# A two-block fp32 transformer on one core: the scan's state products on column halves, one bank per attention head, and the order of two mixers

## The chip, the cores and the metric

The kernel runs on 1 core of one Trainium2 chip. The metric is the device time of one execution in microseconds, as the median of several runs.

## What is computed

256 tokens x of width 1024 (and 256 context tokens) go through two blocks in fp32. The first block has two layers. Its layer 0 mixes with a bidirectional gated delta rule (8 heads of 64, chunks of 64 tokens) and with latent attention (MLA, 8 heads); its layer 1 with neighbourhood attention (8 heads) and grouped-query attention (8 heads on 2 key heads). Each layer ends in a gated FFN. The second block has two layers whose mixer joins sparse attention over chosen keys, a causal 31-tap convolution and a pooling. Cut to what the change touches:

```python
# delta rule, per chunk, head and direction
v_new = u_i - w_i @ s
o_i   = qd_i @ s + qk_i @ v_new
s     = s * gl_i + kd_i.T @ v_new

# attentions of the first block, per head
p = softmax(q @ k.T * scale + bias)        # 256 queries, 512 keys
o = p @ v

# second block's mixer
scores = index(qi, ki, wi)                 # per token half; top 64 of up to 256 keys
o_att  = softmax(q @ k.T + mask(top_k(scores))) @ v
y      = conv31(a * sigmoid(g)) + conv_b
o_conv = silu(layernorm(y)) @ conv_pw
out    = concat(o_att, o_conv, o_pool) @ w_out
```

## The kernel before

The program is one long piece of straight code. A scheduler sets the order of the instructions on each engine from the order of the code and its own estimate of durations; each engine then runs its instructions strictly in that order. Products with weights are made of three matmuls on parts of each number (mm3, L554 to L556); the weights stream in as 512 KB transfers, and ScalarE (L270) and VectorE or GpSimd (L272) make the two parts. PSUM has eight banks. Each stage divides them by kind: the layer-0 mixer has three "g" (reached by aux()), two "s", and one each of "tp", "po", "gv"; the layer-1 mixer and the second block's mixers have two "acc" (acc()), two "s", two "tp", one "aux" and one "po". A new tile of a kind waits until its bank's last reader is done.

*Scan (gdn_run, 264 to 396 us).* Four rounds; in each, the forward and the backward direction take one tile of two chunks. gdn_operands makes, by products of 64 by 64 (L1159, L1161) and transposes (L1164), the tile's u, w, decayed keys kd and decayed queries Q. gdn_state then goes through the tile's two chunks, one on partitions 0 to 63, one on 64 to 127 (the "row half" a): w·S for four head pairs (L1193), v_new on VectorE (gvn, L1196), the state update kd·v_new as four matmuls of 64 rows by 128 columns (L1200), of whose 128x128 results only the two diagonal 64x64 blocks are added to S, and Q·v_new as eight matmuls on one quarter of the array (L1211). The backward direction starts after the forward one's chunks in the code. MLA's pairs 0 and 1 and the modulation products are mixed in by the scheduler; MLA's pairs 2 and 3 come behind (396 to 441 us).

*attend.* For a pair of heads and 128 queries: scores into two banks, row maximum on VectorE (L674), exponentials and their sums on ScalarE (p, L676), four transposes per head into a bank of another kind (L679), copies to SBUF (pt, L682 on VectorE, L684 on ScalarE), the products with v (L690). sums_row makes a row of reciprocal sums (L698, L700). In MLA and in the layer-1 mixer p and pt have two buffers each (K.np).

*Layer-1 mixer (l1_mixer).* linear_tok makes blocks (chunk, token tile) of the input product; consume then issues what hangs on them. The order is: chunks 2, 1 and half of 0, na(0), chunk 4 and half of 3, na(1), the late transposes of the grouped-query keys and queries (late, through pairs_T, L1350, each through the one aux bank), gqa(0), gqa(1). na(t) and gqa(t) are four pairs each for 128 queries.

*Second mixers (s_mixer, twice).* Index scores and top-k for token half 1 (choose(1), VectorE, writes the mask at L1630), linears, qkv, then in this order: conv (128 matmuls on diagonal weights that ScalarE makes, L1531, in two banks, the bias as a 32nd tap), choose(0), the pooling, finish (layer norm from L1542 to L1547, transposes L1550, scaling and tanh, the pointwise product L1560, split L652 and L653), att(1), att(0). s_attend takes one head pair's scores on top of mask products (L1645), with p and pt in two buffers each.

Of the kernel before, what the change touches and what calls it, by code (L numbers as in the profile page):

```python
# [10 lines left out]
F32 = mybir.dt.float32  # L11
# [653 lines left out]
def attend(K, score, v, po, rb, c, kinds=("s", "s", "tp", "tp")):  # L665


    nc = K.nc
    sm = cut(K, [128, 2], F32, "sm", 4)
    pts = []  # L670
    for hh, ps in enumerate(score([bank(K, kinds[0]), bank(K, kinds[1])])):
# [9 lines left out]
        if hh:  # L681
            nc.vector.tensor_copy(pt[:, :n], tp[:, :n])  # L682
        else:
            nc.scalar.copy(pt[:, :n], tp[:, :n])  # L684
# [103 lines left out]
def l0_mla(K, O):  # L788
# [49 lines left out]
    wq = None  # L838
    for pair in range(4):
# [21 lines left out]
        for t in range(4):  # L861
            n = 256 if t < 2 else 512

            def score(pss):
                tk = slice(t * 128, (t + 1) * 128)
                for hh in range(2):
# [4 lines left out]
                   ("s", "g", "tp", "g") if late else ("s", "s", "tp", "tp"))  # L871
        nc.scalar.copy(O[:, pair, :], rb)
        nc.vector.tensor_tensor(O[:, pair, :], po, O[:, pair, :], op=ALU.mult)

# [309 lines left out]
def gdn_state(K, d, first, t, a, u, wq, kd, Q, S):  # L1184
    nc = K.nc
    r = slice(64 * a, 64 * a + 64)
    o = slice(64 - 64 * a, 128 - 64 * a)
# [13 lines left out]
    pSv = pS.rearrange("p (q c) -> p q c", q=4)  # L1201
    for hh in range(2):
        x = slice(hh * 64, hh * 64 + 64)
        if first:
            nc.vector.tensor_copy(S[x, :, x], pSv[x, :, x])
        else:
            nc.gpsimd.tensor_tensor(S[x, :, x], S[x, :, x], bc(K.glc[d][x, t, a, :], [64, 4, 64], 2), op=ALU.mult)
            nc.vector.tensor_tensor(S[x, :, x], S[x, :, x], pSv[x, :, x], op=ALU.add)
# [145 lines left out]
def l1_mixer(K, W, oh, ol):  # L1354
# [44 lines left out]
    def na(t):  # L1399
        po, rb = bank(K, "po"), aux(K)  # L1400
        for pair in range(4):
            def score(pss):
                out = pair_scores(K, (qh[:, pair], ql[:, pair]), (kh[:, pair], kl[:, pair]), 512, tok(t), pss)
                for hh in range(2):
# [5 lines left out]
                   ("s", "acc", "tp", "acc") if t == 1 and pair >= 1 else ("s", "s", "tp", "tp"))  # L1410
        attended(K, po, rb, oh, ol, 0, t)

    def gqa(t):
        po, rb = bank(K, "po"), aux(K)
        for pair in range(4):
            g = pair // 2

            def score(pss):
                return pair_scores(K, (gqh[:, pair], gql[:, pair]), (gkh[:, g], gkl[:, g]), 512, tok(t), pss)
            attend(K, score, lambda hh, j: vg[:, j, g * 64:g * 64 + 64], po, rb, pair * 128, ("s", "acc", "tp", "acc"))  # L1420
# [49 lines left out]
def s_conv(K, i, oh, ol):  # L1470
# [46 lines left out]
    def taps(c):  # L1517

        for j in range(32):
            if j % 3 == 0:  # L1520
                dg = cut(K, [128, 3, 128], F32, "dg", 2)
            nc.scalar.mul(dg[:, j % 3, :], K.ident, dw[:, i, c, j:j + 1] if j < 31 else dwb[:, i, c:c + 1])
            yield j, dg[:, j % 3, :]

    def conv():

        ps = [bank(K, "po"), bank(K, "tp")]
        for c in range(2):
            for j, dg in taps(c):
                for t in range(2):  # L1530
                    nc.tensor.matmul(ps[t][:, c * 128:c * 128 + 128],  # L1531
                                     yp[:, c, t * 128 + j:t * 128 + j + 128] if j < 31 else ones, dg,
                                     start=(j == 0), stop=(j == 31))
        return ps

    def finish(ps):
        y = cut(K, [128, 2, 256])
        back = acc(K)
# [94 lines left out]
def s_attend(K, g, t, qh, ql, kh, kl, mask, U, O):  # L1633
# [6 lines left out]
    for hh in range(2):  # L1640
        r = slice(hh * 64, hh * 64 + 64)
        ps = bank(K, "s")
# [6 lines left out]
        p, pt = cut(K, [128, 512], F32, "p", 2), cut(K, [128, 512], F32, "pt", 2)  # L1649
        tp = bank(K, "tp")  # L1650
# [6 lines left out]
        po = bank(K, "po")  # L1657
# [10 lines left out]
def s_mixer(K, W, i, xh, xl, oh, ol):  # L1668
# [37 lines left out]
    with Pool(K, "ix"):  # L1706
# [252 lines left out]
def layer1(K, h):  # L1959
# [5 lines left out]
    with Pool(K, "l1o"):  # L1965
# [8 lines left out]
        closed(K, K.px)  # L1974
        W.drop()
# [40 lines left out]
def second(K, h):  # L2016
# [10 lines left out]
    for i in range(2):  # L2027
        with Pool(K, "so"):
# [8 lines left out]
            closed(K, K.px)  # L2037
            W.drop()
# [132 lines left out]
```

## Time and profile before

| | |
|---|---|
| median of 3 runs | 2148.2 us (2139.5 to 2151.42) |
| the profiled execution | 2141.66 us; its span 2139.8 us |
| mean granted TensorE clock | 0.955 |
| PE busy | 2003.9 us (94%) |
| VectorE, ScalarE, GpSimd busy | 1318.1, 923.5, 241.2 us |

The span is the time from the first to the last instruction of the profiled execution. PE is the matmul engine; its clock has two levels, 2.4 GHz (granted clock 1.00) and 1.2 GHz (0.50), and a stretch's granted clock is the mean over it. DVE is VectorE, ACT is ScalarE, POOL is GpSimd. A row of a timeline gives start and duration in us, then engine, line, operation, tiles, sizes and, in brackets, the idle time ahead of it with what ended it. A matmul of fp32 is two instructions, and a matmul's duration includes the time it needs to drain, so the price of a group is read from its start to the next group's start.

### The profile page before, as it was taken

To read this page: it belongs to the slowest core of one execution; us is meant where nothing else is said; L and a number is where in the kernel's file an instruction comes from. 1 tells how busy PE (TensorE), PEld (TensorE's weight loads), DVE (VectorE), ACT (ScalarE), POOL (GpSimd) and SP (SyncE) were. 2 spreads that over 40 slices of the span, in tenths; PEclk is the share of its full clock that TensorE was granted. 3 is DMA by queue.
4 is the path that set the end of the run, shared out by engine and by line. 5 is a ranking of instruction groups with operands and counts; after the bars stand their busy time and mean duration, and the time that the engine had idled before them with its cause. 6 is when DMAs were issued, how large, how long until landed. Compare 5 with 4: busy or idle time off the path is not lost.

```text
span 2139.8 us, 31171 instructions
## 1 busy us (share of the span) xinstructions
PE 2003.9 (94%) x11656; PEld 1629.7 (76%) x11656; DVE 1318.1 (62%) x2737; ACT 923.5 (43%) x1614; POOL 241.2 (11%) x312
## 2 busy tenths in 40 slices
PE   6989799899999999799798999998999999989998
PEld 3768578678878778687466888997788789868886
DVE  5666557767776744637556555574765557577644
ACT  4533444344222234434445443564554345555532
POOL 2120112301000000213101001110200021020000
PEclk9999899899999999899689999998999999989999
DMA  8344640234686633213024654521556535155662
GB/s 282 94 114 115 197 139 26 69 100 128 190 261 209 191 105 99 91 61 102 25 89 147 188 187 149 159 87 48 189 179 194 168 108 147 31 167 177 187 187 69
DMA packets 186952, 291.90 MB, mean 136 GB/s; under 512 B 28472, under 2 KB 75704, under 8 KB 186800
## 3 DMA queue, kind: packets, MB, share of 16 engines
q1 hardware_dynamic: 172720, 272.54, 40.8%
q0 software_dynamic: 5472, 16.13, 2.2%
q10 hardware_dynamic: 8608, 1.23, 0.4%
q8 instruction: 92, 1.51, 0.3%
q14 instruction: 60, 0.49, 0.1%
HBM read 281.44 MB, written 8.41 MB: 135 GB/s over the span
## 4 chain that ended last, share of the span: by engine, by line
PE 85%; DVE 6%; DMA 4%; ACT 3%; issue 2%; ACTq 0%; POOL 0%; SPq 0%; DVEq 0%; POOLq 0%
PE acc L554 19%; PE acc L556 19%; PE acc L555 19%; PE s L554 2%; PE s L555 2%; PE s L556 2%; PE po L690 2%; PE tp L891 2%; PE po L1531 1%; PE tp L1531 1%; DMA wraw<-in_w_mod_dram 1%; PE gv L373 1%; DVE wlo L272 1%; PE tp L679 1%; PE aux L729 1%
## 5 line engine op out<-in xcount | busy, mean ns | idle before, releaser
L272 DVE TENSOR_TENSOR wlo<-wraw,whi 128x512 fp32r<-128x512 f32 (+4 forms) x772 | 482.0, 669 | 293.6 <-ACT whi L270 276.6
L270 ACT CAST whi<-wraw 128x1024 fp32r<-128x1024 f32 (+4 forms) x420 | 413.4, 990 | 483.7 <-PE acc L556 200.5
L554 PE MATMUL acc<-whi,u 128*128 128x512 f32 (+3 forms) x1320 | 510.2, 389 | 17.8 <-ACT u L306 11.2
L556 PE MATMUL acc<-whi,u 128*128 128x512 f32 (+3 forms) x1320 | 507.0, 386 | 1.2 <-DVE u L307 1.2
L555 PE MATMUL acc<-wlo,u 128*128 128x512 f32 (+3 forms) x1320 | 508.1, 387 | 0.0
L554 PEld LDWEIGHTS acc<-whi,u 128*128 128x128 f32 x1320 | 252.1, 191 | 68.0 <-ACT u L306 13.7
L556 PEld LDWEIGHTS acc<-whi,u 128*128 128x128 f32 x1320 | 251.8, 191 | 51.4 <-DVE u L307 3.6
L555 PEld LDWEIGHTS acc<-wlo,u 128*128 128x128 f32 x1320 | 252.3, 191 | 48.3 <-DVE wlo L272 1.4
L554 PE MATMUL acc<-u,whi 128*128 128x512 f32 (+1 forms) x480 | 170.0, 361 | 1.8 <-ACT u L306 1.7
L556 PE MATMUL acc<-u,wlo 128*128 128x512 f32 (+1 forms) x480 | 170.0, 358 | 0.0
L555 PE MATMUL acc<-u,whi 128*128 128x512 f32 (+1 forms) x480 | 169.5, 355 | 0.2 <-DVE u L307 0.2
L272 POOL TENSOR_TENSOR wlo<-wraw,whi 128x512 fp32r<-128x512 f32 (+1 forms) x68 | 84.0, 1266 | 431.0 <-ACT whi L270 431.0
L432 DVE SCALAR_TENSOR_TENSOR msum<-mraw,u,msum 128x512 f32<-128x512 f32 x140 | 100.8, 747 | 13.7 <-DMA mraw<-in_w_mod_dram 12.7
L554 PEld LDWEIGHTS acc<-u,whi 128*128 128x128 f32 x480 | 90.1, 189 | 17.0 <-issue 2.6
L555 PEld LDWEIGHTS acc<-u,whi 128*128 128x128 f32 x480 | 90.7, 189 | 15.1 <-issue 1.7
L556 PEld LDWEIGHTS acc<-u,wlo 128*128 128x128 f32 x480 | 90.3, 189 | 15.1 <-issue 1.7
L307 DVE TENSOR_TENSOR u<-aux,u 128x512 fp32r<-128x512 f32 (+2 forms) x96 | 59.5, 632 | 40.6 <-ACT u L306 40.4
L306 ACT CAST u<-aux 128x512 fp32r<-128x512 f32 (+2 forms) x96 | 50.3, 542 | 52.4 <-PE aux L729 36.5
L554 PE MATMUL acc<-whi,dxh 128*128 128x512 f32 x176 | 69.7, 396 | 1.9 <-ACT dxh L306 1.9
L555 PE MATMUL acc<-wlo,dxh 128*128 128x512 f32 x176 | 69.6, 396 | 0.0
L556 PE MATMUL acc<-whi,dxl 128*128 128x512 f32 x176 | 68.7, 396 | 0.0
L307 DVE TENSOR_TENSOR dxl<-u,dxh 128x1024 fp32r<-128x1024 f32 x22 | 26.7, 1224 | 52.8 <-ACT dxh L306 52.8
(511 smaller groups left out, 3103.1 us busy)
## 6 DMA issues: line engine op xcount, KB each, us to landing
wraw<-in_w_up_dram SPq DMA_DIRECT2D x64, 512.0 KB, 4.0
wraw<-in_w_down_dram SPq DMA_DIRECT2D x64, 512.0 KB, 3.9
mraw<-in_w_mod_dram SPq DMA_DIRECT2D x56, 512.0 KB, 4.9
wraw<-in_w_ffn_down_dram SPq DMA_DIRECT2D x44, 512.0 KB, 3.8
wraw<-in_w_mod_dram SPq DMA_DIRECT2D x40, 512.0 KB, 5.7
wraw<-in_w_ffn_gate_dram SPq DMA_DIRECT2D x48, 256.0 KB, 3.0
wraw<-in_w_ffn_up_dram SPq DMA_DIRECT2D x48, 256.0 KB, 3.6
wraw<-in_w_ffn_gate_dram SPq DMA_DIRECT2D x20, 512.0 KB, 3.7
```

The costliest lines, as they stand in the source:

```text
L270: self.K.nc.scalar.copy(hi, raw)
L272: e.tensor_tensor(lo[:, k], raw[:, k], hi.bitcast(F32)[:, k], op=ALU.subtract)
L306: (hi_eng or nc.scalar.copy)(hi, src)
L307: nc.vector.tensor_tensor(lo, src, hi.bitcast(F32), op=ALU.subtract)
L373: nc.tensor.matmul(ps[32 * j:32 * j + 32, :], K.cl[:, g + k, :], raw[:, k, :], start=(g + k < 4), stop=(g + k >= 4))
L432: nc.vector.scalar_tensor_tensor(accs[s], raw[:, k, :], c, accs[s], op0=ALU.mult, op1=ALU.add)
L554: mm(ps, ah, bh, start=start, stop=False)
L555: mm(ps, ah, bl, start=False, stop=False)
L556: mm(ps, al, bh, start=False, stop=stop)
L690: nc.tensor.matmul(po[hh * 64:hh * 64 + 64, c:c + 128], v(hh, j), pts[hh][0][:, j * 128:(j + 1) * 128], start=(j == 0), stop=(j == nj - 1))
L891: nc.tensor.matmul(tp[:, t * 128:(t + 1) * 128], x[:, t // 2, t % 2 * 128 + j:t % 2 * 128 + j + 128], dg[j], start=(j == 0), stop=(j == 4))
L1531: nc.tensor.matmul(ps[t][:, c * 128:c * 128 + 128], yp[:, c, t * 128 + j:t * 128 + j + 128] if j < 31 else ones, dg, start=(j == 0), stop= ...
```

## The change

In the scan, the state update is eight products of 64 by 64 that alternate between the two column halves of the array and fill 256 columns of one bank. Both directions' operands come ahead of both directions' state steps. The query products of both directions are issued alternately, head by head, into one bank, on two diagonal quarters of the array. In attend, a head's transposes go into the bank that held its scores (tp = bks[hh]), so that a head uses one bank, and pairs rotate over the kinds; p and pt get three buffers in MLA and six in the layer-1 mixer. There the linears all come first, then na(0), the late transposes, na(1), gqa. In the second mixers att(1) is ahead of the convolution, finish and att(0) behind it; s_attend uses one bank per head too, with p and pt in four buffers, and the convolution fits in one bank, with its bias as one matmul ahead of the taps.

```diff
 def attend(K, score, v, po, rb, c, kinds, copies="SV"):
+    bks = [bank(K, kinds[0]), bank(K, kinds[1])]
+    for hh, ps in enumerate(score(bks)):
...
-        tp = bank(K, kinds[2 + hh])
+        tp = bks[hh]
...
-def gdn_state(K, d, first, t, a, u, wq, kd, Q, S):
+def gdn_state(K, d, first, t, a, u, wq, kd, S):
...
         nc.vector.tensor_tensor(vn[r], u[r], ps[r], op=ALU.subtract)
-    pS, po = aux(K), aux(K)
+        gdn_o(K, t, a, slice(64 - 64 * a, 128 - 64 * a), ps)
+    pS = aux(K)[:, :256].rearrange("p (q c) -> p q c", q=4)
     for p in range(4):
-        c = slice(p * 128, (p + 1) * 128)
-        nc.tensor.matmul(pS[:, c], kd[r, c], vn[r, c], start=True, stop=True)
+        for hh in range(2):
+            c = slice(p * 128 + hh * 64, p * 128 + hh * 64 + 64)
+            nc.tensor.matmul(pS[hh * 64:hh * 64 + 64, p, :], kd[r, c], vn[r, c], start=True, stop=True)
...
-    for h in range(8):
-        hs = slice(h * 64, h * 64 + 64)
-        nc.tensor.matmul(po[o, hs], Q[r, h, :], vn[r, hs], start=True, stop=True)
-    if not first:
-        gdn_o(K, t, a, o, ps)
-    gdn_o(K, t, a, o, po)
+    return vn
...
 def gdn_run(K):
     for i in range(4):
-        for d in range(2):
-            t = i if d == 0 else (1, 0, 3, 2)[i]
-            ops = gdn_operands(K, d, t)
-            for a in ((0, 1) if d == 0 else (1, 0)):
-                gdn_state(K, d, i == 0 and a == d, t, a, *ops, K.S[d])
+        ts = [i, (1, 0, 3, 2)[i]]
+        ops = [gdn_operands(K, d, ts[d]) for d in range(2)]
+        for s in range(2):
+            vns = []
+            for d in range(2):
+                u, wq, kd, Q = ops[d]
+                a = s ^ d
+                vns.append((64 * a, Q, gdn_state(K, d, i == 0 and s == 0, ts[d], a, u, wq, kd, K.S[d])))
+            po = aux(K)
+            for h in range(8):
+                hs = slice(h * 64, h * 64 + 64)
+                for a, Q, vn in vns:
+                    K.nc.tensor.matmul(po[64 - a:128 - a, hs], Q[a:a + 64, h, :], vn[a:a + 64, hs], start=True, stop=True)
...
@@ l1_mixer @@
-    linear_tok(K, W, xs, w, chunks, [(2, 0), (2, 1), (2, 2), (2, 3), (1, 0), (1, 1), (1, 2), (1, 3), (0, 2), (0, 3)],
-               consume)
-    na(0)
-    linear_tok(K, W, xs, w, chunks, [(4, t) for t in range(4)] + [(3, 2), (3, 3)], consume)
-    na(1)
-    for f in late:
-        f()
-    for t in range(2):
-        gqa(t)
+    linear_tok(K, W, xs, w, chunks, [(2, 0), (2, 1), (2, 2), (2, 3), (1, 0), (1, 1), (1, 2), (1, 3), (0, 2), (0, 3),
+                                     (4, 0), (4, 1), (4, 2), (4, 3), (3, 2), (3, 3)], consume)
+    closed(K, K.px)
+    W.drop()
+    with Pool(K, "at"):
+        K.np = 6
+        na(0)
+        for f in late:
+            f()
+        na(1)
+        for t in range(2):
+            gqa(t)
...
@@ s_mixer @@
         qkv()
-        cv = conv()
-        choose(0)
-        pool_out(0)
-        pool_out(1)
-        finish(cv)
-        att(1)
-        att(0)
+        with Pool(K, "at"):
+            att(1)
+            cv = conv()
+            choose(0)
+            pool_out(0)
+            pool_out(1)
+            finish(cv)
+            att(0)
```

Three places on PE, where the scheduler's order shows what moved. A row reads: line, operation, tile written, tiles read, size, and how many.

The end of na(1) in the layer-1 mixer, before: the last products with v (L690), the late transposes (L1350; lkd are doubled keys), then the first scores of gqa (L710).

```order
L690 MATMUL po_9058<-pt_9239,u_8091 64x128
L1350 MATMUL aux_9257<-const_id_75,lkd_8760 128x128 x2
L1350 MATMUL aux_9262<-const_id_75,lkd_8810 128x128 x2
L1350 MATMUL aux_9267<-const_id_75,lkd_8866 128x128 x2
L1350 MATMUL aux_9272<-const_id_75,lkd_8922 128x128 x2
L1350 MATMUL aux_9277<-const_id_75,lx_8977 128x128 x4
L710 MATMUL s_9294<-u_8087,u_8089 128x512
L710 MATMUL acc_9295<-u_8087,u_8089 128x512
```

The same place now, in the middle of na(1) (L709 scores, L681 transposes of p, L689 products with v, L1366 late transposes):

```order
L709 MATMUL acc_9208<-u_8107,u_8109 128x512
L709 MATMUL acc_9208<-u_8108,u_8109 128x512
L709 MATMUL acc_9208<-u_8107,u_8110 128x512
L681 MATMUL tp_9116<-const_id_75,p_9141 128x128 x4
L681 MATMUL s_9161<-const_id_75,p_9177 128x128 x4
L1366 MATMUL aux_9078<-const_id_75,lkd_8585 128x128 x2
L709 MATMUL tp_9253<-u_8107,u_8109 128x512
L709 MATMUL tp_9253<-u_8108,u_8109 128x512
L709 MATMUL tp_9253<-u_8107,u_8110 128x512
L681 MATMUL s_9162<-const_id_75,p_9187 128x128 x4
L689 MATMUL po_9112<-pt_9137,u_8115 64x128
```

The late transposes stood in a row; now each stands between the work of several pairs, whose scores are already in three kinds of bank.

The end of qkv in the first of the two second mixers, before (L1531 is the convolution; the s products behind it are the index scores of token half 0):

```order
L555 MATMUL acc_12548<-wlo_12517,u_9657 128x384
L556 MATMUL acc_12548<-whi_12516,u_9658 128x384
L1531 MATMUL tp_12615<-dg_12626,u_11691 128x128
L1531 MATMUL po_12614<-dg_12626,u_11691 128x128
...
L1531 MATMUL tp_12615<-dg_12636,u_11691 128x128
L554 MATMUL s_12831<-u_12037,u_12066 128x128
L555 MATMUL s_12831<-u_12038,u_12066 128x128
```

The same place now (L1366 are the transposes of att(1)'s keys and queries, L1677 its mask products, the s products its scores):

```order
L555 MATMUL acc_12544<-wlo_12513,u_9653 128x384
L556 MATMUL acc_12544<-whi_12512,u_9654 128x384
L1366 MATMUL aux_12586<-const_id_75,akd_12576 128x128 x2
L1366 MATMUL aux_12591<-const_id_75,u_11681 128x128 x4
L1366 MATMUL aux_12598<-const_id_75,akd_12584 128x128 x2
L1677 LDWEIGHTS u_11652
L1677 MATMUL s_12614<-u_11685,u_11652 128x256
...
L1366 MATMUL aux_12603<-const_id_75,u_11681 128x128 x4
L554 MATMUL s_12614<-u_12024,u_12026 128x256
L555 MATMUL s_12614<-u_12025,u_12026 128x256
```

The convolution behind the linears is gone from here, and att(1) has taken its place.

The end of the same mixer, before (L1550 and L1560 belong to finish, L1655, L1660 and L729 to the attentions, the last row to w_out):

```order
L1550 MATMUL acc_12955<-const_id_75,lnx_12981 128x128 x2
L1655 MATMUL tp_13109<-const_id_75,p_13107 128x128 x4
L1660 MATMUL po_13057<-u_11685,pt_13048 128x64 x4
L1655 MATMUL tp_13146<-const_id_75,p_13144 128x128 x2
L1560 MATMUL aux_12995<-u_12954,u_11698 128x256
...
L1655 MATMUL tp_13224<-const_id_75,p_13222 128x128 x2
L1660 MATMUL po_13178<-u_11685,pt_13171 128x64 x2
L1660 MATMUL po_13204<-u_11685,pt_13197 128x64 x2
L729 MATMUL aux_13236<-const_id_75,u_12032 128x128 x2
L1660 MATMUL po_13230<-u_11685,pt_13223 128x64 x2
L729 MATMUL aux_13236<-const_id_75,u_12032 128x128 x2
L554 MATMUL acc_13295<-whi_13268,u_11661 128x512
```

The same place now (L1563 is the convolution, L1687 and L1692 are att(0), L1582 and L1592 finish, L728 att(0)'s output):

```order
L1692 MATMUL acc_13196<-u_11681,pt_13190 128x64 x2
L1563 MATMUL po_12737<-dg_12948,u_11687 128x128 x2
L1687 MATMUL tp_13202<-const_id_75,p_13214 128x128 x2
L1692 MATMUL acc_13221<-u_11681,pt_13215 128x64 x2
L1582 MATMUL aux_13077<-const_id_75,lnx_13099 128x128 x2
L1582 MATMUL aux_13077<-const_id_75,lnx_13103 128x128 x2
L1592 MATMUL aux_13117<-u_13076,u_11694 128x256 x2
L1592 MATMUL aux_13122<-u_13076,u_11694 128x256 x2
L728 MATMUL aux_13227<-const_id_75,u_12028 128x128 x4
L554 MATMUL acc_13286<-whi_13259,u_11657 128x512
```

The attentions' last units stood behind the transposes of finish; now they stand ahead of them, and finish has only the four transposes of L728 beside it.

## Rows read from the trace of the kernel before

**Rows 1.** The page: busy time of each engine; the chain's shares by engine.
```profile
PE 2003.9 (94%) x11656; PEld 1629.7 (76%) x11656; DVE 1318.1 (62%) x2737; ACT 923.5 (43%) x1614; POOL 241.2 (11%) x312
...
PE 85%; DVE 6%; DMA 4%; ACT 3%; issue 2%; ACTq 0%; POOL 0%; SPq 0%; DVEq 0%; POOLq 0%
```

**Rows 2.** Windows: length, busy PE, PEld, DVE, ACT, POOL, then PE clock, DMA share, GB/s.
```profile
264.00:396.00 132.00, 124.78 (x1384) 100.10 (x1381) 89.39 (x169) 50.29 (x117) 26.45 (x39) 0.97 0.25 79
376.00:400.00 24.00, 20.46 (x181) 17.35 (x178) 16.21 (x37) 5.06 (x11) 8.69 (x14) 0.73 0.23 69
396.00:441.00 45.00, 40.37 (x252) 28.93 (x250) 34.49 (x66) 23.73 (x57) 10.46 (x14) 0.95 0.23 80
973.00:1105.00 132.00, 113.56 (x646) 78.48 (x646) 83.55 (x207) 58.23 (x121) 25.11 (x40) 0.80 0.14 44
1012.00:1105.00 93.00, 74.56 (x403) 49.28 (x398) 51.15 (x97) 38.32 (x82) 11.20 (x13) 0.72 0.07 22
1050.00:1083.00 33.00, 31.43 (x120) 20.36 (x120) 12.93 (x18) 9.99 (x24) 0.00 (x0) 0.50 0.00 1
1464.00:1490.00 26.00, 19.85 (x94) 17.00 (x92) 12.61 (x43) 7.44 (x23) 1.14 (x2) 0.67 0.03 11
1866.00:1890.00 24.00, 17.85 (x95) 14.94 (x95) 14.57 (x46) 8.94 (x24) 1.14 (x2) 0.77 0.13 41
```

**Rows 3.** Timeline of PE in the scan: start, duration, engine, line, operation.
```profile
279.13 0.68 PE L1161 MATMUL g<-u,gke 64*64 64x64 f32 x16
279.74 0.33 PE L1164 MATMUL g<-const_id,gqe 128*128 128x128 f32 x1
...
284.75 1.14 PE L1211 MATMUL g<-gu,gQ 64*64 64x64 f32 x16
285.82 1.16 PE L1193 MATMUL g<-u,gwq 128*128 128x128 f32 x8
...
289.87 1.16 PE L1200 MATMUL g<-gvn,gkd 64*128 64x128 f32 x8
290.96 0.97 PE L1211 MATMUL g<-gvn,gQ 64*64 64x64 f32 x13
...
291.88 0.98 PE L1159 MATMUL g<-u,u 64*64 64x64 f32 x27
```

**Rows 4.** Groups of L1200 and L1211: count, ns min/median/max, first and last start.
```profile
L1200 PE MATMUL g<-gvn,gkd x112: 272/272/579, 274.0 to 393.1; 64*128 64x128 f32 x112
...
L1211 PE MATMUL g<-gvn,gQ x224: 218/218/363, 275.1 to 395.1; 64*64 64x64 f32 x112
```

**Rows 5.** Waits of PE, 1010 to 1105 us: total, times, longest in us.
```profile
PE tp L679 <- ACT p L676: 6.7, 4, 2.8
```

**Rows 6.** Timeline of PE, 1040 to 1050 us.
```profile
1044.20 0.44 PE L1350 MATMUL aux<-const_id,lkd 128*128 128x128 f32 x2 [0.92 <-DVE u L307]
1045.56 0.44 PE L1350 MATMUL aux<-const_id,lkd 128*128 128x128 f32 x2 [0.92 <-DVE u L307]
```

**Rows 7.** Timelines of PE and DVE at the end of qkv, first second mixer.
```profile
1416.64 0.34 PE L556 MATMUL acc<-whi,u 128*128 128x384 f32 x1
1416.81 0.38 PE L1531 MATMUL tp<-dg,u 128*128 128x128 f32 x2
...
1423.00 0.43 DVE L1630 TENSOR_TENSOR u<-u,const_rest 128x256 bf16<-128x256 f32 x1
```

**Rows 8.** Timelines of DVE and PE at the end of the same mixer.
```profile
1463.92 0.43 DVE L1542 BATCH_NORM_STATS2 bst<-po 128x6 f32<-128x256 f32 x1 [1.08 <-PE po L1531]
...
1467.86 0.53 DVE L1547 TENSOR_SCALAR lnx<-tp,bmv,rsy 128x256 f32<-128x256 f32 x1
...
1481.77 0.42 DVE L653 SCALAR_TENSOR_TENSOR u<-aux,u 128x256 fp32r<-128x256 f32 x1 [2.06 <-ACT u L652]
...
1468.00 0.69 PE L1550 MATMUL acc<-const_id,lnx 128*128 128x128 f32 x2 [3.35 <-DVE lnx L1547]
...
1489.76 0.80 PE L554 MATMUL acc<-whi,u 128*128 128x512 f32 x1 [1.62 <-ACT whi L270]
```

More of the change, by code (lines that the diff above doesn't have):

```diff
@@ L661, in heads_T, with attend @@
     feat_split(K, hi, lo, ps[:, :T * 128], scale)
-def attend(K, score, v, po, rb, c, kinds=("s", "s", "tp", "tp")):
+def attend(K, score, v, po, rb, c, kinds, copies="SV"):
     nc = K.nc
@@ L670, in attend @@
     pts = []
-    for hh, ps in enumerate(score([bank(K, kinds[0]), bank(K, kinds[1])])):
+    bks = [bank(K, kinds[0]), bank(K, kinds[1])]
+    for hh, ps in enumerate(score(bks)):
         n = ps.shape[-1]
@@ L680, in attend @@
         pt = cut(K, [128, 512], F32, "pt", K.np)
[L681 to L684, printed above, removed]
+        (nc.vector.tensor_copy if copies[hh] == "V" else nc.scalar.copy)(pt[:, :n], tp[:, :n])
         pts.append((pt, n // 128))
@@ L838, in l0_mla, with unit @@
     wq = None
+    used = [0]
+    def unit(kinds):
+        used[0] += 2
+        return [kinds[(used[0] + i) % len(kinds)] for i in range(2)]
+    K.np = 3
     for pair in range(4):
@@ L870, in l0_mla @@
             attend(K, score, lambda hh, j: vt[:, j, pair * 128 + hh * 64:pair * 128 + hh * 64 + 64], po, rb, t * 128,
-                   ("s", "g", "tp", "g") if late else ("s", "s", "tp", "tp"))
+                   unit(("s", "s", "tp", "g", "g", "g") if late else ("s", "s", "tp")))
         nc.scalar.copy(O[:, pair, :], rb)
         nc.vector.tensor_tensor(O[:, pair, :], po, O[:, pair, :], op=ALU.mult)
+    K.np = 2
 def gdn_conv(K, W, f0, nf, silu, tensor):
@@ L1409, in na @@
             attend(K, score, lambda hh, j: vn[:, j, pair * 128 + hh * 64:pair * 128 + hh * 64 + 64], po, rb, pair * 128,
-                   ("s", "acc", "tp", "acc") if t == 1 and pair >= 1 else ("s", "s", "tp", "tp"))
+                   unit(), "SS")
         attended(K, po, rb, oh, ol, 0, t)
@@ L1419, in score, with unit @@
                 return pair_scores(K, (gqh[:, pair], gql[:, pair]), (gkh[:, g], gkl[:, g]), 512, tok(t), pss)
[L1420 removed]
+            attend(K, score, lambda hh, j: vg[:, j, g * 64:g * 64 + 64], po, rb, pair * 128, unit())
         attended(K, po, rb, oh, ol, 4, t)
[L1423 to L1431 removed]
+    used = [0]
+    def unit():
+        used[0] += 1
+        return [("s", "acc", "tp")[used[0] % 3]] * 2
+    linear_tok(K, W, xs, w, chunks, [(2, 0), (2, 1), (2, 2), (2, 3), (1, 0), (1, 1), (1, 2), (1, 3), (0, 2), (0, 3),
[10 more added lines that the diff above has]
+            gqa(t)
+        K.np = 2
 def rope2_tables(K, pool):
@@ L1517, in taps @@
     def taps(c):
-        for j in range(32):
+        for j in range(31):
             if j % 3 == 0:
                 dg = cut(K, [128, 3, 128], F32, "dg", 2)
-            nc.scalar.mul(dg[:, j % 3, :], K.ident, dw[:, i, c, j:j + 1] if j < 31 else dwb[:, i, c:c + 1])
+            nc.scalar.mul(dg[:, j % 3, :], K.ident, dw[:, i, c, j:j + 1])
             yield j, dg[:, j % 3, :]
     def conv():
-        ps = [bank(K, "po"), bank(K, "tp")]
+        ps = bank(K, "po")
+        bias = cut(K, [128, 2, 256], F32, "pt", 4)
+        for t in range(2):
+            for c in range(2):
+                nc.scalar.mul(bias[:, t, c * 128:c * 128 + 128], K.ident, dwb[:, i, c:c + 1])
+        nc.tensor.matmul(ps, ones, bias.rearrange("p t f -> p (t f)"), start=True, stop=False)
         for c in range(2):
@@ L1530, in conv @@
                 for t in range(2):
[L1531 to L1534, printed above, removed]
+                    nc.tensor.matmul(ps[:, t * 256 + c * 128:t * 256 + c * 128 + 128],
+                                     yp[:, c, t * 128 + j:t * 128 + j + 128], dg,
+                                     start=False, stop=(c == 1 and j == 30 and t == 1))
+        return [ps[:, t * 256:t * 256 + 256] for t in range(2)]
     def finish(ps):
         y = cut(K, [128, 2, 256])
-        back = acc(K)
+        back = aux(K)
         mv = cut(K, [128, 2, 2], F32, "bmv", 1)
@@ L1641, in s_attend @@
         r = slice(hh * 64, hh * 64 + 64)
-        ps = bank(K, "s")
+        ps = bank(K, ("s", "tp")[hh])
         for x in range(2):
@@ L1648, in s_attend @@
         nc.vector.tensor_reduce(nmx, ps[:, :2 * n].rearrange("p (x s) -> p x s", x=2), axis=AX.X, op=ALU.max, negate=True)
-        p, pt = cut(K, [128, 512], F32, "p", 2), cut(K, [128, 512], F32, "pt", 2)
-        tp = bank(K, "tp")
+        p, pt = cut(K, [128, 512], F32, "p", 4), cut(K, [128, 512], F32, "pt", 4)
+        tp = ps
         for x in range(2):
@@ L1656, in s_attend @@
         (nc.vector.tensor_copy if hh else nc.scalar.copy)(pt[:, :2 * n], tp[:, :2 * n])
-        po = bank(K, "po")
+        po = acc(K)
         for x in range(2):
```

15 lines of the change are left out of this document (7 added, 8 removed).

## The prediction

> **What bounds the kernel now.** I read the page first: TensorE (PE) is busy for 94% of the span and makes up 85% of the chain of work that ended last [rows 1]. So time comes from three places only: PE work that goes away, PE idle time, and PE work done at the lower of its two clocks (1.2 instead of 2.4 GHz, granted clock 0.50 instead of 1.00). Next I cut the program into the stretches that the change touches and read for each the busy time and the granted clock [rows 2]. Length less busy time is idle; busy time times (1 − clock) is what the low clock cost. The scan (264 to 396 us) is nearly full: 7.2 us idle, clock 0.97, so there only less work helps, except in its tail (376 to 400), which has 3.5 us idle and 20.46 × 0.27 = 5.5 us of clock loss. The layer-1 mixer's attentions (973 to 1105) are another picture: 18.4 us idle and 113.56 × 0.20 = 22.7 us lost to the clock. In 1050 to 1083 PE is busy for 31.43 of 33 us, all of it at 0.50: a dense stretch, but a slow one, after the idle time ahead of it. The ends of the two second mixers (1464 to 1490, 1866 to 1890) show 6.2 us idle each, with clocks 0.67 and 0.77.
>
> The profiled execution took 2141.7 us, 6.5 us less than the median of the runs shown (2148.2). The sum is made against 2141.7. About 0.5% (11 us) is what a measurement of this kernel can tell from no change.
>
> **Scan: less work.** A state update (L1200) is 4 matmuls in 8 instructions of 128 columns, though only the diagonal 64-blocks of its result are used; it takes from 289.87 to 290.96, 1.09 us [rows 3]. The new one is 8 matmuls, 16 instructions of 64 by 64, which stay on one row half and alternate the column half of the array. The nearest row is the operands' product of the same form (L1161, 16 instructions): 279.13 to 279.74, 0.61 us [rows 3]. There are 112 + 16 such instructions in all, 16 updates ([rows 4] show the 112 of the steps after the first): 16 × 0.48 = 7.7 us less.
>
> The query products (L1211) are 16 instructions per direction on one quarter of the array, 284.75 to 285.82, 1.07 us, 67 ns each [rows 3]; 224 + 32 of them make 16 groups [rows 4]. The change issues both directions' 32 alternately on two diagonal quarters into one bank. The nearest row is L1159, which alternates two diagonal quarters of one bank as well: 27 instructions in 0.98 us, 36 ns [rows 3]. A pair costs 32 × 36 ns = 1.16 us instead of 2.14, eight times: 7.8 us less. What would undo it is that two row halves could not write one bank side by side; then 67 ns stays and the gain is nothing. The row says they can, so I take 7.8. Beside it, the Trainium skill ("TensorEngine Tiling (Array Packing)", Gotcha 1: PSUM Pressure) states that different row tiles write to different banks and cannot use the same bank simultaneously; by that the sum would be 7.8 us higher, and this trace speaks against it, since L1159 does just that at 36 ns.
>
> VectorE's work in the scan hardly changes (the output adds are as many), and it is busy 89 of 132 us [rows 2], so PE stays the bound. Computing both directions' operands ahead of both state steps lets one direction's chain (w·S, subtraction on VectorE, update, addition) hide the other's: in the tail I take back 5 of the 9 us. The MLA pairs behind it (396 to 441) have 4.6 us idle and 2 us of clock loss [rows 2]; with three to six banks in rotation and three p/pt buffers I take back 2. Scan and MLA: −7.7 − 7.8 − 5 − 2 = **−22 us**; bounds −8 (update alone) and −31 (everything back).
>
> **Layer-1 mixer: order and banks.** PE's work at full clock is 113.56 × 0.80 = 91 us in 132. The idle time is mostly one wait: the transposes of a head wait 6.7 us for the exponentials on ScalarE (p, L676) [rows 5], since at most two heads are in flight and nothing else is queued. In the changed order all linear chunks come first, and each head holds one bank instead of two, so three pairs are in flight. The late key transposes (L1350), before one after the other at the end of na(1) with 1.36 us from one start to the next for 0.44 us of work [rows 6], now stand between pairs of na(1). What the move costs: na(0) loses its cover, the six blocks of chunks 4 and 3. The attention work of all 16 pairs is about 71 us of PE, an estimate from 74.56 × 0.72 = 54 us after 1012 [rows 2], the work of about 12 pairs; 54/12 × 16 = 71. For those 54 us VectorE was busy 51.15 and ScalarE 38.32 us [rows 2], other work than attention among it. So PE remains the bound, narrowly, if the pairs overlap. I keep 8 us idle (first pair, last pair, the first weights of w_out, which are loaded and cast as late as before) and 8 us at the low clock, of 41: 107 us, **−25 us**. Bounds: 0 (what is won at one end is lost in na(0)) and −36.
>
> **Second mixers: the cover moves.** Here the change costs. The last qkv product starts at 1416.64 and convolution matmuls follow it at once, while VectorE runs the top-k of token half 1, whose mask is written at 1423.00 + 0.43 [rows 7]. In the changed order att(1) stands at this place and the convolution behind it; PE's queue is in order, so what waits for the mask holds the convolution too. VectorE is full up to the mask, so it comes no earlier. Between 1416.9 and 1423.4 PE has three rounds of transposes through the one aux bank (2, 4 and 2 transposes, 1.8 us by the 0.44 us of a round of two [rows 6]): 5 us idle. The last round and its two casts come behind the mask products: 1 more. Then four head units with only each other as cover: 1. With 2 us of low clock that is 9 us. The later half gains and loses: att(0) now runs under the convolution, but finish ends the mixer alone. Its chain is 4.5 us from the statistics (1463.92) to the second normalised tile (1467.86 + 0.53) [rows 8], then transposes, scaling, tanh, products and splits, which took until 1482.19 (1481.77 + 0.42) with attention between them and which I put at 7, an estimate from their own durations. The tail before had 26 − 19.85 × 0.67 = 12.7 us without work at full clock [rows 2]; the new one has about 9 idle and 3 of low clock in w_out: 12, no difference. So +9 each, **+18 us** for two; bounds 0 (the mask's wait covered by an earlier end of the index scores) and +16 each.
>
> The bias of the convolution as one 512-column matmul instead of four, with two more ScalarE products, goes under ScalarE's free time there: nothing, at most 1 us either way. Weight prefetch for w_out still hangs on the same releases: nothing.
>
> **Sum.** 2141.7 − 22 − 25 + 18 = 2112.7; I say **2112 us**.
>
> **Rivals.**
> *The low clock stays in layer 1* (chance 0.19). For: 1050 to 1083 was dense attention and stayed at 0.50 for 33 us [rows 2]. Against: the MLA pairs (396 to 441), attention too, ran at 0.95. Layer 1 gains only some 5 us: 2132.
> *The shared bank serialises the query products* (0.10): 67 ns each, 2120. Against it stands L1159. This is what the rule of the Trainium skill ("TensorEngine Tiling (Array Packing)", Gotcha 1) would come to here.
> *The second mixers lose nothing* (0.15): the scheduler's rotation of banks lets scores start early and the tail shrinks by the moved attention: 2095.
> *The scan is bound elsewhere* (0.04): the wait of PE for VectorE's subtraction grows by what PE saves; only layer 1 moves: 2135.
> *Slower* (0.09): in layer 1 the attentions, uncovered, open gaps from the first pair on, PE falls to 1.2 GHz and stays there as after 1050. All 71 us of attention work at half clock: 91 + 71 + 8 = 170 us instead of 132, +38; with −22 and +18 that is 2176. It decides from a layer-1 mixer of 136 us, that is, when 37 of the 71 us run at half clock. For it: 33 us of wall time did. Against: the gaps that came ahead of that stretch (the serial L1350 rounds) are filled now.
> My forecast has 0.43.
>
> **How the numbers follow.** The likeliest case alone spans 2097 to 2128 (second mixers 0 to +32, layer 1 −10 to −36, partly cancelling). The range reaches down to the better bounds, −31 and −36 with +5 for the second mixers (2080), and up to layer 1 at nothing with the second mixers at +26 (2146). Faster by over 0.5% (below 2137): the forecast, the bank rival, the lossless second mixers, and about a third of the low-clock rival: 0.74. Within 0.5%: the rest of that rival and the scan bound elsewhere: 0.16. Slower: the last rival, and a hundredth for both second mixers at +16 with layer 1 at nothing: 0.10.
>
> **What would show it.** In the profile after: update rows of 16 instructions at 0.6 us; rows of 32 query products at 1.1 to 1.2 us (2.1 if the bank serialises); the scan with MLA over some 22 us sooner. Layer-1 attentions in about 107 us with clock above 0.9; if 0.5 stands there for 30 us or more, the first or the last rival holds. In the second mixers 5 to 7 us of idle PE ahead of the score products, with the mask's VectorE row as releaser, and a tail of 11 to 12 us from the last convolution matmul to w_out. I am wrong if the second mixers lose over 16 us each, or if layer 1 takes over 136 us.

## The result, and the profile after

The changed kernel took 2125.68 us (median of 7, 2120.47 to 2135.06), before it 2148.2 us (median of 7); the ratio is 0.9904 (95% interval 0.9885 to 0.9923), so 1.0% faster. The forecast was 2112 within 2080 to 2146. In a second set of 8 executions it took 2130.14 us against 2146.0 (0.9926, 0.9901 to 0.9951). Expected of that set were a median near 2126 and second mixers of less than 90 us each in its profile; they took 86.3 and 86.1. The execution profiled with the first set was its longest (2135.06), the one of the second set its shortest (2121.39 of 2121.39 to 2144.49). The lines below are of the latter (span 2119.6), and the first one is used for what differs between the two: by its span of 2133.3 us the change won 6.5 us, by that of the second 20.2.

The page of the changed kernel, busy times and the chain (before: [rows 1]):

```profile
PE 1970.3 (93%) x11772; PEld 1602.7 (76%) x11772; DVE 1312.7 (62%) x2729; ACT 930.2 (44%) x1626; POOL 241.9 (11%) x312
...
PE 83%; DVE 6%; DMA 5%; ACT 3%; issue 2%; POOL 1%; SPq 0%; ACTq 0%; DVEq 0%; POOLq 0%
```

PE is still what the end hangs on, and 33.6 us of its busy time are gone, though the span is only 20.2 us shorter. To see where the rest went I took the same landmarks on PE in both timelines: the start of the last group of products of the scan's inversion, the first w_out product of each mixer, and the last qkv product of each second mixer.

| stretch, us | before | after | change | forecast |
|---|---|---|---|---|
| inversion to w_out of layer 0 (scan, MLA) | 181.2 | 159.4 | −21.8 | −22 |
| to w_out of layer 1 (FFN, layer-1 mixer) | 662.6 | 639.3 | −23.3 | −25 |
| to the end of qkv, second mixer 1 | 311.8 | 310.4 | −1.4 | 0 |
| to its w_out | 73.1 | 86.3 | +13.2 | +9 |
| to the end of qkv, second mixer 2 | 328.3 | 322.8 | −5.6 | 0 |
| to its w_out | 69.2 | 86.1 | +16.9 | +9 |
| to the end | 252.5 | 254.1 | +1.6 | 0 |

Two of the three terms came as forecast; the third, the second mixers, gave back 30.1 us, not 18. Of the 5.6 us between the two second mixers some 3 are the clock (granted 0.93 in the 50 us from 1689.76 before, 1.00 in the same 50 us after, from 1656.67), and fourteen convolution instructions no longer stand ahead of the landmark. The windows over these stretches, of before first (columns as in [rows 2]; they are not the same cuts as there):

```profile
261.10:442.30 181.20, 168.05 (x1770) 131.75 (x1769) 127.84 (x247) 77.72 (x181) 36.92 (x52) 0.96 0.25 81
1417.00:1489.80 72.80, 66.65 (x467) 57.84 (x466) 36.47 (x130) 36.98 (x115) 1.14 (x2) 0.88 0.08 25
1818.40:1887.30 68.90, 62.75 (x468) 54.58 (x466) 36.63 (x131) 35.72 (x114) 1.14 (x2) 0.94 0.09 25
```

and of the changed kernel: the two second mixers, the top and the tail of the first of them, layer 1's attentions, scan with MLA:

```profile
1370.70:1456.70 86.00, 70.02 (x475) 58.39 (x475) 39.48 (x137) 40.89 (x126) 1.15 (x2) 0.84 0.10 31
1779.80:1865.50 85.70, 70.10 (x475) 58.65 (x475) 39.08 (x137) 39.59 (x125) 1.15 (x2) 0.84 0.10 32
1370.70:1402.00 31.30, 23.88 (x140) 19.13 (x140) 17.09 (x55) 14.08 (x41) 0.00 (x0) 0.73 0.06 18
1440.00:1456.70 16.70, 8.24 (x32) 5.06 (x31) 7.99 (x29) 3.21 (x7) 1.15 (x2) 0.67 0.18 63
957.00:1060.00 103.00, 91.72 (x631) 67.79 (x629) 78.08 (x198) 60.16 (x127) 27.21 (x43) 0.90 0.18 56
261.30:420.70 159.40, 145.77 (x1898) 112.33 (x1897) 123.87 (x244) 77.10 (x181) 37.67 (x52) 0.99 0.28 92
```

Busy time times clock is the work at full clock: in the second mixers 58.7 and 59.0 us before, 58.8 and 58.9 after. The work is the same as far as a clock of two decimals can tell (0.35 us); all of the loss is idle time and the low clock. Idle time rose from 6.2 and 6.2 to 16.0 and 15.6, the clock's loss from 8.0 and 3.8 to 11.2 and 11.2.

**The scan's products.** The timeline of PE in the changed kernel:

```profile
303.67 0.51 PE L1209 MATMUL g<-gvn,gkd 64*64 64x64 f32 x10
303.96 0.27 PE L1237 MATMUL g<-gvn,gQ 64*64 64x64 f32 x1
...
304.18 1.09 PE L1237 MATMUL g<-gvn,gQ 64*64 64x64 f32 x29
305.20 0.38 PE L1200 MATMUL g<-u,gwq 128*128 128x128 f32 x1
...
308.48 0.68 PE L1209 MATMUL g<-gvn,gkd 64*64 64x64 f32 x16
309.09 0.38 PE L1200 MATMUL g<-u,gwq 128*128 128x128 f32 x1
```

An update alone is 308.48 to 309.09, 0.61 us, as costed. An update with the 32 query products behind it, 48 instructions, is 303.67 to 305.20, 1.53 us or 32 ns each (1.54 and 1.55 in two other groups, 2.45 in one at a granted clock of 0.57; the rest have other products mixed in). A step of both directions costs 2.14 us where it cost 2 × (1.09 + 1.07) = 4.32 [rows 3]: 17.4 us less over eight.

**The top and the tail of a second mixer.** The timeline of PE after the last qkv product (1370.33):

```profile
1370.33 0.34 PE L556 MATMUL acc<-whi,u 128*128 128x384 f32 x1
1373.76 0.58 PE L1366 MATMUL aux<-const_id,akd 128*128 128x128 f32 x2 [3.09 <-DVE akd L1733]
1376.11 1.12 PE L1366 MATMUL aux<-const_id,u 128*128 128x128 f32 x4 [1.77 <-DVE u L307]
1378.64 0.69 PE L1366 MATMUL aux<-const_id,akd 128*128 128x128 f32 x2 [1.41 <-DVE u L653]
1379.82 0.37 PE L1677 MATMUL s<-u,u 128*128 128x256 bf16 x1 [0.49 <-DVE u L1662]
...
1380.63 1.06 PE L1366 MATMUL aux<-const_id,u 128*128 128x128 f32 x4
1382.37 0.58 PE L554 MATMUL s<-u,u 64*128 64x256 f32 x1 [0.69 <-ACT u L652]
```

and behind the last convolution matmuls (L1563):

```profile
1440.31 0.66 PE L1563 MATMUL po<-dg,u 128*128 128x128 f32 x4
1440.81 0.38 PE L1687 MATMUL tp<-const_id,p 128*128 128x128 f32 x2
1442.15 0.66 PE L1692 MATMUL acc<-u,pt 128*128 128x64 f32 x4 [0.96 <-DVE pt L1688]
1445.22 1.14 PE L1582 MATMUL aux<-const_id,lnx 128*128 128x128 f32 x4 [2.40 <-DVE lnx L1579]
1447.95 2.05 PE L1592 MATMUL aux<-u,u 128*128 128x256 f32 x4 [1.59 <-issue]
1450.93 2.07 PE L1592 MATMUL aux<-u,u 128*128 128x256 f32 x4 [0.93 <-DVE u L653]
1453.94 1.12 PE L728 MATMUL aux<-const_id,u 128*128 128x128 f32 x4 [0.93 <-DVE u L653]
1456.67 0.80 PE L554 MATMUL acc<-whi,u 128*128 128x512 f32 x1 [1.62 <-ACT whi L270]
```

Where the convolution ran back to back before [rows 7], PE now stops five times in 12 us ahead of att(1)'s scores, 7.45 us in all, and at the end finish runs alone, with six stops of 8.4 us.

How far one trace can be trusted shows in the kernels of the experiments below, each profiled once (the change itself twice). The same stretches, by the same landmarks:

| stretch, us | kernels without the part | kernels with it |
|---|---|---|
| inversion to w_out of layer 0 | 181.2 (before), 186.6, 188.7, 189.7 | 159.3 to 166.1 (ten traces) |
| to w_out of layer 1 | 662.6 (before), 657.4, 659.3 | 635.7 to 640.6 (ten traces) |
| both second mixers, qkv to w_out | 142.3 (before), 137.6 to 142.2 (four) | 168.9, 172.4, 180.5 |
| between the two | 328.3 (before), 325.1 to 329.5 (four) | 321.5, 322.8, 324.4 |

All ranges lie apart. By their means the parts are −24, −21, +33 and −5 us. The scan's stretch in the trace that the forecast was made from was the shortest of four.

### The profile page after: what moved, and what is told of

The parts are those of the page before. It is cut to its first block, busy times and chain, and to the rows that moved or that the text cites. A ratio compares the mean times of both kernels' runs of the same rounds, so it can differ in the third digit from the quotient of the medians.

```text
span 2133.3 us, 31383 instructions
## 1 busy us (share of the span) xinstructions
PE 1980.7 (93%) x11772; PEld 1610.4 (75%) x11772; DVE 1311.8 (61%) x2729; ACT 929.1 (44%) x1626; POOL 242.3 (11%) x312
## 4 chain that ended last, share of the span: by engine, by line
PE 79%; DVE 7%; DMA 7%; ACT 3%; issue 2%; POOL 1%; ACTq 0%; SPq 0%; DVEq 0%; POOLq 0%
PE acc L554 18%; PE acc L555 18%; PE acc L556 18%; PE po L1563 3%; PE s L554 2%; PE s L555 2%; PE s L556 2%; PE po L689 2%; DVE wlo L272 2%; PE gv L373 1%; DMA mraw<-in_w_mod_dram 1%; DMA wraw<-in_w_mod_dram 1%; ACT whi L270 1%; PE aux L489 1%; PE aux L728 1%
## 5 line engine op out<-in xcount | busy, mean ns | idle before, releaser
L1563 PE MATMUL po<-dg,u 128*128 128x128 f32 x496 | 64.0, 283 | 0.2
```

Source lines behind the costliest of these rows:

```text
L1563: nc.tensor.matmul(ps[:, t * 256 + c * 128:t * 256 + c * 128 + 128], yp[:, c, t * 128 + j:t * 128 + j + 128], dg, start=False, stop=(c == ...
```

## The experiments

Each kernel ran beside the kernel before on the same chip; medians and ratios are to that one's (2150.56 us in the first four, 2143.51 in the next four, 2146.0 in the next three, 2144.0 in the last).

**1. The three parts alone, and the change without its new order in the second mixers.**

scan_only takes gdn_state and gdn_run alone into the kernel of before; l1_only takes l1_mixer with its one-bank heads; mixers_only takes s_conv, s_attend and s_mixer.

> The kernel of before with the scan's part alone (gdn_state, gdn_run). Theory A: the products' 16 us of TensorE work leave the path, and little of the tail: 2130 us (between 2128 and 2134). Rival B: part of the 17 us that the traces show for scan and MLA comes from MLA's banks, and the scan is held by VectorE: 2140 or more.

Measured: 2126.67 us, ratio 0.9897 (0.9856 to 0.9937), 24 us less; the stretch from the inversion to w_out is 160.8 us, against 181.2 before and 159.4 with the whole change. The execution profiled was much the fastest of five (2106.34; the others 2123.65 to 2128.12), so its span is not used. MLA's new banks are not needed for the gain: 160.8 lies within the 159.3 to 166.1 of the kernels that have them.

> The kernel of before with layer 1's part alone (all linears first, late transposes between na(0) and na(1), one bank per head, six buffers). Theory A: this is an independent stage, 28 us less: 2120 us. Rival B: the clock's level at the start of the attentions depends on what came before; then less than 15 us is won and layer 1 shows 0.5 over 30 us or more.

Measured: 2121.97 us, 0.9872 (0.9837 to 0.9908), 28.6 us less; layer 1's stretch is 636.3 us, as in the kernels that have the other parts too (635.7 to 640.6). The part is independent of the others.

> The kernel of before with the second mixers' part alone. Theory A: it costs what the rest wins back: 22 us (by the medians) to 35 us (by the two profiles) more, 2170 to 2183. Rival B: the loss seen in the profiles is an accident of the clock in one execution, and the part costs less than 10 us: below 2158.

Measured: 2167.0 us, 1.0095 (1.0057 to 1.0133), 16 us more; from the end of qkv to w_out 84.1 and 84.8 us, together 26.6 more than before. The loss is real, and not an accident of one execution, though less than the 38 us by which the two stretches grew in the first profile of the change.

The fourth kernel is the changed one with one piece of s_mixer put back:

```diff
-            att(1)
             cv = conv()
             choose(0)
             pool_out(0)
             pool_out(1)
             finish(cv)
+            att(1)
             att(0)
```

> The changed kernel with the second mixers' order of before (convolution, index scores of half 0, pooling, finish, then both attentions), their new banks and buffers kept. Theory A: the two mixers lost time because att(1) stands at the top without the convolution as cover and because finish ends them alone; the order back gives 2100 us (the scan's 17 and layer 1's 28 us stay), and the stretch from the end of qkv to w_out comes back to some 73 us from 94. Rival B: the loss comes from the shared banks (a head's transposes wait for its own scores, only two kinds for all heads); then the order alone gives nothing back and it stays near 2125.

Measured: 2102.05 us, 0.9786 (0.9753 to 0.9819). Theory A: the order alone gives back some 24 us. The two stretches are 74.4 and 74.6 us.

**2. Which part of the second mixers' order, and what the banks do there.**

> The changed kernel with the second mixers whole as before (order, banks, buffers, convolution in two banks): scan, MLA and layer 1 alone are changed. Theory A: the order is the whole loss; about the same as with the order alone back (2102), within 5 us. Rival B: the one-bank heads and the four buffers are worth something of their own in these mixers: 2108 or more. Rival C: they cost something too (the two stretches were 74 us long with the order back, and 68 to 73 in kernels that leave the mixers alone): 2095.

Measured: 2093.32 us, 0.9757 (0.9716 to 0.9798): nearest to rival C. Its windows from qkv to w_out, then those of the kernel above, with the old order but the new banks and the convolution in one bank:

```profile
1377.00:1449.30 72.30, 66.16 (x467) 57.33 (x465) 36.34 (x130) 36.97 (x115) 1.14 (x2) 0.90 0.08 25
1777.40:1846.30 68.90, 62.77 (x466) 54.48 (x465) 36.29 (x130) 35.70 (x114) 1.15 (x2) 0.94 0.08 26
```

```profile
1371.30:1445.30 74.00, 67.86 (x470) 57.54 (x470) 36.27 (x132) 40.32 (x125) 1.15 (x2) 0.88 0.11 37
1771.50:1845.80 74.30, 68.37 (x471) 57.95 (x470) 36.13 (x132) 39.39 (x124) 1.15 (x2) 0.87 0.11 36
```

The idle time is about the same (6.1 and 6.1 against 6.1 and 5.9 us), and the work at full clock too (59.5 and 59.0 against 59.7 and 59.5); the clock's loss is 6.6 and 3.8 us against 8.1 and 8.9. In the second kernel the attentions are through before finish is, which then ends the mixer alone, as in the change. So in the traces the mixers' new banks cost some 7 us in the two stretches, of which 2 come back between them (325.9 against 327.7). In the time a price is not shown: the intervals of 0.9786 and 0.9757 overlap, and another pair of these kernels, with att(1) ahead of finish in both, stands at 0.9783 with the new banks and 0.9773 with the old ones (both below). This version, scan, MLA and layer 1 without any of the second mixers' changes, has the lowest median of all the kernels here: 2.4% under before, where the change itself is at 1.0%.

> The changed kernel with att(1) behind the convolution, the index scores of half 0 and the pooling, and ahead of finish and att(0). Theory A: the convolution again covers the mask, and finish's chain on VectorE lies between two attentions: 2100, as with the order of before, or up to 5 us less. Rival: att(1)'s VectorE and ScalarE work ahead of finish delays its chain, which then ends alone: 2106 or more.

Measured: 2098.7 us, 0.9783 (0.9752 to 0.9815); 74.4 and 73.1 us. Theory A.

> The changed kernel with the convolution alone moved ahead of att(1); att(1) stays ahead of the index scores of half 0. Theory A: the gap at the top goes (5 to 7 us of idle PE per mixer and the half clock behind it), but the top-k of half 0 now has only att(1) as cover and att(0) ends the mixer behind it: between 2102 and 2115. Rival: if the top is not what costs, it stays at 2122 or more.

Measured: 2114.03 us, 0.9852 (0.9818 to 0.9886); 80.8 and 80.1 us. Theory A: the convolution alone, put back at the top, is worth about half of what the whole order is (the two stretches fall from 172.4 to 160.9 us, with the whole order to 148.9); the rest lies in what follows. There finish leaves PE idle while the top-k of half 0 is not yet through:

```profile
1431.66 1.08 PE L1582 MATMUL aux<-const_id,lnx 128*128 128x128 f32 x4 [3.35 <-DVE lnx L1579]
1434.41 2.05 PE L1592 MATMUL aux<-u,u 128*128 128x256 f32 x4 [1.67 <-issue]
1437.39 2.07 PE L1592 MATMUL aux<-u,u 128*128 128x256 f32 x4 [0.93 <-DVE u L653]
1440.00 0.29 PE L1677 MATMUL s<-u,u 128*128 128x128 bf16 x1 [0.54 <-DVE u L1662]
```

**3. What holds PE at the top.** The prediction said: VectorE's top-k, up to the mask. So I took most of it away; this kernel chooses 8 keys instead of 64 for token half 1 and leaves the others out of the result.

```diff
-    for _ in range(8):
+    for _ in range(1 if t else 8):
```

> The changed kernel in its own order, with one round of the top-k in place of eight for token half 1 (8 keys are chosen, not 64, so that part of the result is left out; some 6.5 us less VectorE work per mixer). Theory A: the gap at the top comes from VectorE, which is full of top-k and mixes it into the work on keys and queries that the transposes wait for; without it PE's idle time there falls from 7 to 3 us or less per mixer and the half clock behind it shortens: 2110 or less. Rival: the four rounds through the one aux bank hold PE by themselves: 2120 or more.

Measured: 2122.84 us, 0.9895 (0.9858 to 0.9931): theory A falls. PE at the top:

```profile
1374.61 0.28 PE L1677 MATMUL s<-u,u 128*128 128x256 bf16 x1
...
1376.67 0.44 PE L1366 MATMUL aux<-const_id,akd 128*128 128x128 f32 x2 [1.45 <-DVE akd L1733]
1378.23 1.12 PE L1366 MATMUL aux<-const_id,u 128*128 128x128 f32 x4 [1.12 <-DVE u L307]
1380.76 0.69 PE L1366 MATMUL aux<-const_id,akd 128*128 128x128 f32 x2 [1.41 <-DVE u L653]
1382.36 1.11 PE L1366 MATMUL aux<-const_id,u 128*128 128x128 f32 x4 [0.92 <-DVE u L307]
```

The mask products (L1677) now run at once, and still the four rounds through the one aux bank hold PE: 5.6 us idle with a last 0.69 ahead of the scores, of 7.45. So I gave the rounds a second bank.

```diff
-            pairs_T(K, U[:, t, 0:512], 4, qh, ql, tk, 0.125)
+            pairs_T(K, U[:, t, 0:512], 4, qh, ql, tk, 0.125, acc(K))
```

> The changed kernel with the query transposes of qkv in the second mixers put into an acc bank, so that the four rounds of att(1) go through two kinds of bank instead of one. Theory D (formed after the run with one round of top-k): the gap at the top is the chain of four rounds through one aux bank, each waiting for ScalarE's and VectorE's reading of the one before; then the waits of L1366 fall from some 6 us to 3 or less per mixer and the time to 2112 to 2120. Rival: the keys' and queries' rotation on VectorE (akd) and the mask set the moment of the scores anyway; 2122 or more, and the wait moves to the mask or to akd.

Measured: 2137.8 us, 0.9955 (0.9938 to 0.9973): theory D falls as well.

```profile
1376.03 1.09 PE L1366 MATMUL acc<-const_id,u 128*128 128x128 f32 x4 [3.28 <-DVE u L1359]
1376.91 0.64 PE L1366 MATMUL aux<-const_id,akd 128*128 128x128 f32 x2
1378.12 1.09 PE L1366 MATMUL acc<-const_id,u 128*128 128x128 f32 x4 [0.58 <-ACT u L306]
1379.89 0.69 PE L1366 MATMUL aux<-const_id,akd 128*128 128x128 f32 x2 [0.68 <-DVE u L307]
1383.18 0.37 PE L1677 MATMUL s<-u,u 128*128 128x256 bf16 x1 [2.60 <-DVE u L1662]
```

The waits between rounds are short now, but what they gave goes to the mask: 2.60 us on L1662, VectorE's last operation of the top-k. Idle time is 7.1 us. The mask itself comes 1.3 us later, since VectorE now makes both splits of the queries (L653) ahead of it. So two chains end within two or three microseconds of each other, the top-k with its mask and the rounds with their casts: from the last qkv product to the first scores it is 12.0 us in the change, 9.7 without most of the top-k and 11.1 with two banks. Each alone holds PE for nearly as long. What helped is cover, as the order back shows. This kernel's median is some 8 us above the change's (2130.14 in the same set), but the intervals of the two ratios overlap, so that it is slower is not shown.

**4. The tail, and layer 1's order without its banks.**

> Scan, MLA and layer 1 of the changed kernel, the second mixers of before, but with att(1) ahead of finish. If finish's chain on VectorE is what leaves PE idle at the end (3.4 us and the half clock behind it, twice), work of att(1) queued ahead of it fills that: 2086. Rival: finish then ends the mixer by itself, as with the new banks: 2098.

Measured: 2098.27 us, 0.9773 (0.9754 to 0.9792), no better than with finish first (2093.32 in another set): PE is idle for 3.45 us again, now ahead of att(1)'s products with v, until the lnx that reads po. In these mixers those products go into the bank po, and that holds the convolution's result until finish has normalised it. So att(1) can't fill that time from in front either, and finish's last split (L653) comes last but for the transposes to w_out. The time is the rival's.

> The kernel of before with layer 1's new order alone (all linears first, late transposes between na(0) and na(1)); the heads keep two banks, the old rotation, the copies on two engines and two buffers. Theory A: the order without the banks uncovers na(0) while only two heads are in flight, so the waits for p grow: 2146 or more, and the 26 us of layer 1 come from the banks. Rival B: the order alone brings most of it, since the late transposes no longer stand in a row and the half clock behind them goes: 2130 or less.

Measured: 2139.16 us, 0.9973 (0.9943 to 1.0003), 5 us less, within what can be told from no change: between the two theories, nearer to A by the time. The waits of PE for the exponentials in the layer-1 attentions of before (the group beside that of [rows 5]), of this kernel and of the changed one:

```profile
PE acc L679 <- ACT p L676: 3.0, 3, 1.7
```

```profile
PE tp L679 <- ACT p L676: 8.3, 6, 2.0
PE acc L679 <- ACT p L676: 1.5, 3, 0.6
```

```profile
PE acc L681 <- ACT p L678: 3.9, 3, 3.3
PE s L681 <- ACT p L678: 2.6, 2, 1.4
...
PE tp L681 <- ACT p L678: 0.4, 1, 0.4
```

With two heads in flight the order alone leaves 9.8 us of waiting for the exponentials, as many as before (9.7): they did not grow, as theory A had it. With one bank per head, six buffers and na's copies on ScalarE it is 6.9. Layer 1's stretch is 662.6 us before (657.4 to 662.6 in the kernels without the part), 651.8 with the order alone and 639.3 with the whole change. So by the traces the order has 6 to 11 us of it and what comes on top 12.5, by the medians 5 of 28.6; the median's 5 is not clear of noise, and this kernel's scan, which the edit leaves alone, was 7.5 us longer in its trace than in that of before. The banks without the order were not run.

## Why the prediction was right, and where its sum was off

**Scan: less work.** Right. The update costs 0.61 us as taken from L1161. The query products cost less than taken, since update and query products together run at 32 ns: 17.4 us of work went instead of 15.5. (The 36 ns was read from a duration, with its drain; from L1159's start to the next group's it is 0.91 us for 27, 34 ns.) The rival that the shared bank serialises them is out: two row halves write one bank at 32 ns an instruction, where a single quarter took 67 [rows 3]. That is also where the Trainium skill ("TensorEngine Tiling (Array Packing)", Gotcha 1: PSUM Pressure), by which different row tiles cannot use one bank simultaneously, does not describe what this kernel does. The other part, 5 us from the tail and 2 from MLA, was partly wrong in kind: PE's idle time in scan and MLA did not fall, it is 13.2 us before and 13.6 after; what fell was the low clock's loss, from 168.05 × 0.04 = 6.7 to 145.77 × 0.01 = 1.5. The work at full clock fell by 17.0 us, as the rows of the products have it, and no wait for VectorE took its place, so the scan is not bound elsewhere. That the total, −21.8, hit the −22 to 0.2 us is luck: the same stretch varies by some 8 us among the kernels that leave it alone. scan_only shows that none of it needs MLA's banks.

**Layer 1.** Right in size: −23.3 (−28.6 alone) for −25. The attentions kept 11.3 us idle and 91.72 × 0.10 = 9.2 us of low clock, where I had kept 8 and 8; their 103 us hold 82.5 us of work, not the 91 of the sum, since more of the linears stand ahead of them. I credited the order of linears and late transposes together with the banks; l1_order shows no gain from the order that is clear of noise in the time, 6 to 11 us in the trace, so at least half of the term is the single bank per head with the buffers and copies. The rival that the clock stays at 0.5 there did not come (0.90, which is some 20 of the 103 us at half clock).

**Second mixers.** Right in direction, and in the gaps at the top, too small in size: +30.1 in this profile (38 in the first) for +18. By the mixer it is 13.2 and 16.9 us here and 20.9 and 17.3 in the first profile, so the sign of being wrong that I had set, over 16 us each, was met in the first profile and not in the second. Idle time at the top was forecast at 7 us and measured at 7.45, though not by the chain I named alone (experiment 3: mask and rounds end within three microseconds of each other). The mask's row ended only 0.49 us of it, the keys' copies and the casts of the rounds 6.3; and the mask came later than before, 9.4 us after the start of the last qkv product instead of 6.8 [rows 7]. The tail was forecast at 12 us without work, as before it; it is 16.70 − 8.24 × 0.67 = 11.2. **The term that failed is "With 2 us of low clock that is 9 us".** At the top the clock cost 23.88 × 0.27 = 6.4 us here, and in the first profile of the same kernel 13.7:

```profile
1374.30:1412.00 37.70, 30.52 (x131) 25.11 (x131) 17.10 (x55) 13.13 (x38) 0.00 (x0) 0.55 0.05 15
```

There all of att(1), its scores, transposes and products, ran at 1.2 GHz, from the first gaps until some 1411, though PE was busy almost without a break from 1386 on. I had used that very picture, 1050 to 1083 [rows 2], for a rival in layer 1, and not for the place where I had just put 7 us of gaps.

**The sum.** −22 −25 +18 = −29 was forecast against the profile; it came out at −6.5 in the first profile, −20.2 in the second and −22.5 and −15.9 in the medians. By medians the parts alone give −24, −28.6 and +16, together −36. That need not mean that the parts work against each other: the three share one median of before, 2150.56, where the other sets have 2143.5 to 2148.2, and against 2146 they would add up to −22. By the stretches of the table they add up to −17. The second mixers cost 32 to 37 us in the medians between the change and the kernel without them, and 27 to 38 in the two stretches of the traces; what differs there from one execution of the same kernel to the next is the clock's level at their top.

## What to carry to other kernels

A unit of work that is long and independent is worth most where several short chains would otherwise leave the main engine waiting; moving it away costs the gaps, and then the low clock over the dense work behind them, which was here 6.4 us in one execution and 13.7 in another for 7 us of gaps. So put a price on the clock at every place where a change opens gaps, from the slowest such stretch in the trace. Take a change of many parts apart: the kernel without one of its three parts was 2.4% faster than before, with it 1.0%.

## What was not expected of the hardware

After some 12 us with five gaps, PE stayed at 1.2 GHz through dense work for about 25 us in one execution, and in another of the same kernel for some 7 (granted clock 0.55 over 37.7 us, 0.73 over 31.3). And 64 by 64 products that alternate over column halves or diagonal quarters of the array run at 32 to 38 ns an instruction, even when both quarters write one bank, against 67 ns on a single quarter.
